# Hybrid decoder layer on one core: gemms by halves in one lasting PSUM layout, branch sums by accumulating transfers, late operand forms inside the first attention-output pair

## The chip, the core and the metric

The kernel runs on one core of one Trainium2 chip. The time is device microseconds of one execution, as the median of several runs. TensorE is called PE, VectorE DVE, ScalarE ACT, GpSimd POOL and the queue engine SyncE SP, as in the profile.

## What is computed

One layer of a hybrid decoder for 1024 prompt tokens and 8 sample tokens, model width 1024, all in float32. Three token mixers (a short gated convolution, a state-space scan "SSD", and a cross-attention into 256 memory tokens) read the same normalized input through one projection `w_in`; their outputs are weighted by gates, summed, multiplied by `w_merge_o` and added to the input; a gated feed-forward block and a last norm follow.

```python
def mixer_block(xn, ...):
    sc_b, sc_c, sc_x, z, xbc, dt_raw, q, gates = jnp.split(xn @ w_in, splits, axis=-1)
    ...
    y_a = (sc_b * conv_u) @ w_sc_out
    ...
    y_b = group_rmsnorm(y_ssd, ssm_norm_w, SSM_GROUPS) @ w_ssm_out
    ...
    y_c = jnp.einsum('bhlm,bmhd->blhd', probs, mem_v).reshape(bsz, seq, ATTN_DIM) @ w_attn_o
    g_a, g_b, g_c = jnp.split(jax.nn.sigmoid(gates), N_BRANCHES, axis=-1)
    merged = g_a * y_a + g_b * y_b + g_c * y_c
    return merged @ w_merge_o, (...)
```

## The kernel before

**Tiling.** Activations lie with features on 128 partitions and tokens along the free axis: eight tiles ("k-tiles") of 128 x 1032 for a width of 1024, where 1032 is the 1024 prompt columns and the 8 sample columns (`TT`; a half, `HT`, is 516). Every float32 operand of TensorE is split into a high and a low part (names that end in `h` and `l`: a cast on ACT, a subtraction on DVE, lines L167/168 for weights, L177/178 for activations, L254/255 and L393/395 in the pairs), and a product is three matmuls: high x high, high x low, low x high.

**Two kinds of products.** `gemm` (L199 to L219) multiplies one block of 128 output features: for each of the eight k-tiles and each of the three operand pairs it runs three matmuls of 260, 512 and 260 columns (`THIRDS`) into one PSUM tile of three banks, from a pool `pmm` of two such tiles. It is used 34 times: two z blocks early, eight q blocks (`q_step`), and 24 output blocks (`out_part`). The other kind is `strassen`, which does two output blocks at once, over halves of the tokens and of the features, with seven products of 24 matmuls in place of eight; its accumulators are three two-bank tiles m0, m1, m2 of a pool `pst`, and its matmuls have 256 and 260 columns. Its operands are combinations of tokens halves ("forms": B11, T1, nT2, B21, T3, B22, T4) and of weights (A, S, T, D: the weights' tiles are called `ao0A`, `ao0S` and so on for the pair `ao0`). The two PSUM pools do not fit side by side, so they are closed and opened in turn: gemms, pairs, gemms, pairs.

**Stages.** Up to 84 us norms and first products; 84 to 980 Strassen pairs for most of `w_in`; 980 to 1140 the q gemms; 1140 to 1551 the 24 output gemms; 1551 to 1655 the attention-output pairs `ao0`, `ao2`, `ao4`, `ao6`; 1655 to 1750 the merge product `pm` (16 blocks of 48 matmuls on half columns); then the feed-forward block.

**What sets the order.** Between the products of the q and output gemms the scan and then the attention run as small pieces: `tick` takes the next piece from a queue, `pace` says how many there are for each gemm, and `gemm` spreads them over its eight k-steps. `out_part(i, m)` runs in three passes of eight blocks m: i = 0 over the convolution branch, gated and written to DRAM as `mg_d`; i = 1 and i = 2 over the two halves of the scan branch, whose sum (L1497), gated (L1498), is written to DRAM as `yg_d`. `owed` holds that write until the next gemm. Each pass reads new operands `b00` to `b07`. The places where they change (`wo00`, `wo10`, `wo20`) are called seams here: `between`, called at each k of the gemm before, splits the first six, and the last two are split when the new pass begins.

**The sample attention.** Its last products are `pso` (L1665, 32 transfers of 1 KB to `os_d`); `s_back` reads them back as `osr` (SP, L1679), transposes them on TensorE into `psob` (L1682) and copies them into the last 8 columns of the eight raw attention tiles (L1685). The forms T1 and nT2 need these columns; after the last gemm (`wo27`) come T3, B22 and T4 (L1832, L1838 and the splits at L395), all in one block before `strassen` for `ao0` is called.

**The pairs and the sum of branches.** In each pair, in the hook `mid`, two gate tiles `gt3` and two tiles `yg` are loaded, and GpSimd adds `mg_d` into each `yg` by an accumulating transfer from DRAM. When the pair's products are done, VectorE multiplies by the gates (L1859, L1862, L1864) and adds `yg` (L1860, L1863, L1865):

```python
V.tensor_mul(oo[1][:, c1], oo[1][:, c1], gts[1][:, c1])
V.tensor_add(merged[m + 1][:, c1], oo[1][:, c1], ygs[1][:, c1])
V.scalar_tensor_tensor(oo[1][:, c0], pa, -1.0, gts[1][:, c0], op0=ALU.mult, op1=ALU.mult)
V.tensor_add(merged[m + 1][:, c0], oo[1][:, c0], ygs[1][:, c0])
```

Each engine and each queue runs its instructions in order; the tile layer puts in the waits and shifts instructions within limits. The merge's operands are the splits of the eight `merged` tiles (`mgs0` to `mgs7`).

## Time and profile before

| | |
|---|---|
| median of 3 runs | 2445.57 us (2440.04 to 2445.65) |
| profiled execution, its own time | 2446.0 us |
| its span | 2444.3 us |
| mean granted TensorE clock | 0.996 |
| attention-output stage, 1551 to 1655 | PE idle 15.3 of 104 us |
| merge matmuls `pm` | 1656.27 to 1750.25 us |
| q gemms, 980 to 1140 | PE idle 1.2 of 160 us |

The span is the time from the first to the last instruction of one profiled execution, and all positions in microseconds count from its start; the execution's own time is 1.7 us longer. Busy times of PE and of its weight loads (PEld) overlap. A row of the timeline or of the chain of waits gives a start, a duration, the engine, the line of the program and the tiles (out<-in). Durations of matmuls overlap with the next one's, so what a matmul costs is the step from one start to the next.

### The profile page before, as it was taken

The numbers are of one execution on the slowest core, as the hardware profiler recorded it, in microseconds if no ns is written. First come the engines' busy times: TensorE is split into PE (matmuls) and PEld (weight loads), VectorE is DVE, ScalarE is ACT, GpSimd is POOL, SyncE is SP. The second block draws the span as 40 slices with busy tenths as digits, with TensorE's granted clock in tenths as the row PEclk, the third lists the DMA queues.
The fourth block names the chain that finished last, engine by engine and source line by source line (L and its number), as shares of the span: only waits on it lengthen the run. The fifth ranks groups of instructions, "written<-read, shape, count | busy, mean of one in ns | idle before, by whom it ended". The sixth has DMA issues, their size and how long they took to land.

```text
span 2444.3 us, 45555 instructions
## 1 busy us (share of the span) xinstructions
PE 2394.4 (98%) x18812; PEld 2283.4 (93%) x18812; DVE 1647.5 (67%) x2688; ACT 1112.7 (46%) x1792; POOL 111.5 (5%) x171
## 2 busy tenths in 40 slices
PE   8999999999999999999999999899999999999998
PEld 7999999999999999888888887899999999999998
DVE  6744686777777775568687763764777655567865
ACT  6634555455454544657555442333543333343423
POOL 0000000000000000212211000000000000000000
PEclk9999999999999999999999999999999999999999
DMA  6444423444454346679796887575455332354622
GB/s 213 133 157 155 130 91 111 129 139 130 130 152 118 113 122 194 200 225 296 240 295 213 270 309 271 172 205 182 141 179 163 105 106 95 101 182 149 190 86 80
DMA packets 356678, 407.90 MB, mean 167 GB/s; under 512 B 15230, under 2 KB 276462, under 8 KB 356463
## 3 DMA queue, kind: packets, MB, share of 16 engines
q1 hardware_dynamic: 332182, 337.50, 45.0%
q10 hardware_dynamic: 23137, 63.26, 6.8%
q0 software_dynamic: 1152, 4.23, 0.9%
q8 instruction: 148, 2.42, 0.4%
q14 instruction: 59, 0.48, 0.1%
HBM read 288.81 MB, written 116.35 MB: 166 GB/s over the span
## 4 chain that ended last, share of the span: by engine, by line
PE 84%; DMA 6%; DVE 6%; ACT 1%; issue 1%; SPq 0%; DVEq 0%; ACTq 0%; POOLq 0%; POOL 0%
PE po L218 8%; PE pm L1934 4%; PE ps_q L218 3%; PE py L1063 1%; PE pss L1076 1%; PE ps_z L218 1%; DMA yg<-mg_d 1%; PE po L1055 1%; PE G16m L267 1%; PE d00m L267 1%; PE Z2m L267 1%; PE Z14m L267 1%; PE X18m L267 1%; PE Z10m L267 1%; PE Z6m L267 1%
## 5 line engine op out<-in xcount | busy, mean ns | idle before, releaser
L1007 ACT ACTIVATE r<-r,acum 128x128 f32<-128x128 f32 x256 | 79.3, 391 | 2.9 <-DMA r<-ac_d 2.1
L796 DVE SCALAR_TENSOR_TENSOR ax<-u,prm,ax 128x1024 f32<-128x1024 f32 x44 | 56.3, 1280 | 0.0
L948 ACT ACTIVATE st<-st,es 128x128 f32<-128x128 f32 x128 | 41.3, 392 | 22.4 <-DMA st<-in_state_ssm_dram 22.4
L1040 POOL TENSOR_TENSOR xdd<-xdt,decst 128x512 f32<-128x512 f32 x32 | 35.3, 1102 | 284.3 <-DVE xdt L1036 275.9
L1034 DVE TENSOR_TENSOR r<-r,cbm 128x1024 f32<-128x1024 f32 x32 | 39.1, 1223 | 4.3 <-ACT r L1009 2.4
L1059 DVE TENSOR_TENSOR y<-po,ea 128x512 f32<-128x512 f32 x28 | 19.3, 690 | 31.7 <-PE po L1055 31.7
L950 DVE SCALAR_TENSOR_TENSOR st<-sr,dts,st 128x128 f32<-128x128 f32 x128 | 40.3, 346 | 0.4
L1076 PE MATMUL pss<-xdd,bT 128*128 128x512 f32 x64 | 34.5, 620 | 2.2 <-ACT bT L1033 1.7
L954 DVE SCALAR_TENSOR_TENSOR sr<-st,sr 128x128 f32<-128x128 f32 x128 | 35.4, 286 | 1.1
L1063 PE MATMUL py<-r,xdt 128*64 128x128 f32 x512 | 35.0, 279 | 0.0
L1009 ACT ACTIVATE r<-r 128x1024 f32<-128x1024 f32 x32 | 33.8, 1058 | 0.7
L1949 DVE TENSOR_TENSOR x<-pm,xT 128x516 f32<-128x516 f32 x15 | 10.4, 694 | 34.1 <-PE pm L1934 34.1
L1089 POOL TENSOR_TENSOR s<-s,cdec 128x512 f32<-128x512 f32 x28 | 33.1, 1182 | 0.9 <-DVE s L1082 0.7
L1063 PEld LDWEIGHTS py<-r,xdt 128*64 128x64 f32 x512 | 27.3, 136 | 4.4 <-issue 1.0
L1055 PE MATMUL po<-bc,s 128*128 128x128 f32 x224 | 29.6, 275 | 0.0
L1055 PEld LDWEIGHTS po<-bc,s 128*128 128x128 f32 x224 | 28.0, 191 | 1.0
L1627 ACT ACTIVATE pr<-psa,mx 128x256 f32<-128x256 f32 x32 | 14.9, 471 | 30.2 <-DVE mx L1625 30.2
L799 DVE SCALAR_TENSOR_TENSOR ax<-u,prm,ax 128x1032 f32<-128x1032 f32 x22 | 28.3, 1286 | 0.0
L793 ACT ACTIVATE ax<-u,prm 128x1024 f32<-128x1024 f32 x22 | 27.4, 1246 | 1.7 <-DVE u L383 0.4
L1615 DVE SCALAR_TENSOR_TENSOR kc<-kc,qb 128x256 f32<-128x256 f32 x64 | 23.8, 419 | 5.6 <-DMA qb<-qs_d 5.4
L1036 DVE TENSOR_TENSOR xdt<-xp,dtT 128x512 f32<-128x512 f32 x32 | 21.9, 684 | 8.0 <-PE xp L1029 8.0
L1033 ACT COPY bT<-bp 128x128 f32<-128x128 f32 x32 | 8.4, 262 | 38.5 <-DVE cbm L1031 38.5
(9290 smaller groups left out, 9046.0 us busy)
## 6 DMA issues: line engine op xcount, KB each, us to landing
r<-ac_d SPq DMA_DIRECT2D x32, 512.0 KB
gt_d<-G ACTq DMA_DIRECT2D x24, 516.0 KB
gt<-gt_d SPq DMA_DIRECT2D x24, 516.0 KB
xs_d<-ax ACTq DMA_DIRECT2D x22, 516.0 KB
zs<-zs_d SPq DMA_DIRECT2D x16, 516.0 KB
yb_d<-x SPq DMA_DIRECT2D x16, 516.0 KB
in<-yb_d SPq DMA_DIRECT2D x16, 516.0 KB
st<-in_state_ssm_dram SPq DMA_DIRECT2D x32, 256.0 KB
```

The costliest lines, as they stand in the source:

```text
L218: PE.matmul(po, wt[:, ks], xc, start=(k == 0 and i == 0), stop=(k == nk - 1 and i == 2))
L267: PE.matmul(po, wt[:, ks], xc, start=(start and kt == 0 and i == 0), stop=(kt == 3 and i == 2), skip_group_check=True,)
L796: V.scalar_tensor_tensor(acc[:, :T], u[:, j : j + T], w[j], acc[:, :T], op0=ALU.mult, op1=ALU.add)
L948: S.activation(st[:, i], st[:, i], AF.Copy, scale=es[:, g * 4 + i, b : b + 1])
L950: V.scalar_tensor_tensor(st[:, i], rb, dts[:, g * 4 + i, b : b + 1], st[:, i], op0=ALU.mult, op1=ALU.add)
L954: V.scalar_tensor_tensor(rb, st[:, i], 1.0, rc, op0=ALU.mult, op1=ALU.mult, accum_out=ys[:, g * 4 + i, b : b + 1],)
L1007: S.activation(r[:, j, :], r[:, j, :], AF.Relu, scale=-1.0, bias=acum[:, c, h : h + 1])
L1034: V.tensor_tensor(r, r, bc(cbm.unsqueeze(1), [P, HPG, P]), op=ALU.mult)
L1055: PE.matmul(po[:, t * P : (t + 1) * P], state["s"][:, t * P : (t + 1) * P], bcg[1][:, cs], start=True, stop=True,)
L1063: PE.matmul(py[hp : hp + 64, (h // 2) * P : (h // 2 + 1) * P], xdt[:, h * 64 : (h + 1) * 64], r[:, (h % 2) * 4 + h // 2, :], start=True, s ...
L1076: PE.matmul(pss, bT, xdd, start=True, stop=True)
L1934: PE.matmul(po, wt[:, ks], x[:, half * HT + lo : half * HT + hi], start=(k == 0 and i == 0), stop=(k == KD - 1 and i == 2),)
```

## The change

It changes these things:

- **One PSUM layout.** The pool `pst` with m0, m1, m2 is opened once; gemms, pairs, merge and feed-forward take the three accumulators in turn from one deque `accs` (`next_ps`; `strassen` reverses it).
- **Gemms by halves.** `gemm` runs all eight k-tiles for the first 516 columns, then for the second, each product in two matmuls of 256 and 260 columns, so four for 1032 columns; the result is taken out by `put` in halves. Pieces are spread over 16 steps; `between` is called at every other one. The last output gemm (`wo27`) is `joint`: both halves in one pass over k, in two accumulators.
- **The start of the attention pairs.** The first weights of `ao0` are taken up before the forms T1 and nT2 and the last gemm. `s_back` comes one piece earlier.
- **Late forms.** The forms B22 and T4 are made after the T3 product of the first pair (`last_aforms`, called by `after_t3`).
- **Sums by transfers.** GpSimd adds `mg_d` into `yg_d` from DRAM to DRAM: blocks 0 to 3 at the start, 4 and 5, then 6 and 7 behind a pair's last transfer (`added`). For the pairs 0, 2 and 4 another accumulating transfer adds `yg_d` into `merged`; only the last pair loads `yg` and adds it on VectorE.

The core of the diff; not shown are the removal of `thirds` and of the old pools, the z blocks, which change as the q blocks do, and the callers that take `next_ps`:

```diff
@@ -196,27 +184,35 @@
 
     seam, owed = [], []
 
-    def gemm(w, acts, name, width=P, off=0):
-
-        hi, lo = w
-        ps = mm_ps(name)
+    def gemm(w, acts, name, put, joint=False):
+
         nk = len(acts)
         n = int(pace[0] + pace[1])
         pace[1] += pace[0] - n
-        marks = [nk * i // n for i in range(n)]
         between = seam.pop() if seam else None
-        for k, (ah, al) in enumerate(acts):
-            if between is not None:
-                between(k)
-            if k == 1 and owed:
-                owed.pop()()
-            for _ in range(marks.count(k)):
-                tick()
-            ks = slice(k * width + off, k * width + off + P)
-            for i, (wt, x) in enumerate(((hi, ah), (hi, al), (lo, ah))):
-                for po, xc in thirds(ps, x):
-                    PE.matmul(po, wt[:, ks], xc, start=(k == 0 and i == 0), stop=(k == nk - 1 and i == 2))
-        return ps
+        parts = ((0, 1),) if joint else ((0,), (1,))
+        marks = [len(parts) * nk * i // n for i in range(n)]
+        at = 0
+        for hs_ in parts:
+            pss = [next_ps(f"{name}{h}") for h in hs_]
+            for k, (ah, al) in enumerate(acts):
+                if between is not None and at % len(parts) == 0:
+                    between(at // len(parts))
+                if at == 2 and owed:
+                    owed.pop()()
+                for _ in range(marks.count(at)):
+                    tick()
+                at += 1
+                ks = slice(k * P, (k + 1) * P)
+                for i, (wt, x) in enumerate(((w[0], ah), (w[0], al), (w[1], ah))):
+                    for h, ps in zip(hs_, pss):
+                        for po, xc in halves_of(ps, x, h * HT):
+                            PE.matmul(
+                                po, wt[:, ks], xc, start=(k == 0 and i == 0), stop=(k == nk - 1 and i == 2),
+                                skip_group_check=True,
+                            )
+            for h, ps in zip(hs_, pss):
+                put(hv(ps), HS[h])
 
     def wblock(w, col):
...
         return pst[0].tile([P, 2, 512], F32, tag=tag, name=name)
+
+    def next_ps(name):
+        ps = st_ps(accs[0], name)
+        accs.rotate(-1)
+        return ps
 
...
             raw1, raw2 = st_raw(src1, f"{nm}r1"), st_raw(src2, f"{nm}r2")
-        tags = ("m0", "m1", "m2") if count[0] % 2 == 0 else ("m2", "m1", "m0")
-        count[0] += 1
+        tags = tuple(accs)
...
-    pmm[0] = mm_stack.enter_context(tc.tile_pool(name="pmm", bufs=2, space=PSUM))
+    pst_stack = ExitStack()
+    pst[0] = pst_stack.enter_context(tc.tile_pool(name="pst", bufs=1, space=PSUM))
 
 
...
         def s():
-            ps = proj(C_Q + i * P, f"q{i}")
             t = ev_tile(f"q{i}")
-            S.activation(t[:, :TT], flat(ps), AF.Copy, scale=QS)
+            proj(C_Q + i * P, f"q{i}", lambda ps, c: S.activation(t[:, c], ps, AF.Copy, scale=QS))
             G.tensor_copy(qs[:, i, :], t[:, T:TT])
             S.dma_start(q_d[i], t[:, :TT])
...
             out_ahead(nxt)
-        ps = gemm(weights(wblock(w, m * P), f"wo{nm}"), acts, f"po{nm}")
-        if i == 0:
-            V.tensor_mul(gt[:, :TT], flat(ps), gt[:, :TT])
-            owed.append(lambda: SY.dma_start(mg_d[m], gt[:, :TT]))
-        elif i == 1:
+        if i == 1:
             t = ev_tile(f"yr{nm}")
-            S.copy(t[:, :TT], flat(ps))
+
+        def put(ps, c):
+            if i == 0:
+                V.tensor_mul(gt[:, c], ps, gt[:, c])
+            elif i == 1:
+                S.copy(t[:, c], ps)
+            else:
+                V.tensor_tensor(t[:, c], ps, t[:, c], op=ALU.add)
+                V.tensor_mul(t[:, c], t[:, c], gt[:, c])
+
+        gemm(weights(wblock(w, m * P), f"wo{nm}"), acts, f"po{nm}", put, joint=nxt is None and m == KD - 1)
+        if i == 1:
             S.dma_start(yr_d[m], t[:, :TT])
         else:
-            V.tensor_tensor(t[:, :TT], flat(ps), t[:, :TT], op=ALU.add)
-            V.tensor_mul(t[:, :TT], t[:, :TT], gt[:, :TT])
-            owed.append(lambda: SY.dma_start(yg_d[m], t[:, :TT]))
+            dst, src_ = ((mg_d, yg_d)[i // 2][m], (gt if i == 0 else t)[:, :TT])
+            owed.append(lambda: SY.dma_start(dst, src_))
 
     split = []
...
             late += [[(s_out, b)], [(states[b],)] if b < 4 else []]
-        late += [[], [(s_back,)]]
+        late += [[(s_back,)]]
         pieces.extend([] for _ in range(at_ + len(late) - len(pieces)))
...
             run_next(outs)
+        wa = [wblock(a["w_attn_o"][0], m * P) for m in range(KD)]
+        ev_sums = lambda n: ev_tile(n, (P, 1024))
+        begun = st_begin(wa[0], wa[1], "ao0", ev_sums)
...
     fxo = fxo_stack.enter_context(tc.tile_pool(name="fxo", bufs=2))
     afx["T4"] = lambda part, nm: fxo.tile([P, 2, HT], F32R, tag=part, name=nm)
-    pst_stack = ExitStack()
-    pst[0] = pst_stack.enter_context(tc.tile_pool(name="pst", bufs=1, space=PSUM))
-    ev_sums = lambda n: ev_tile(n, (P, 1024))
-    wa = [wblock(a["w_attn_o"][0], m * P) for m in range(KD)]
-    begun = st_begin(wa[0], wa[1], "ao0", ev_sums)
     for kt in range(4):
         b12, b22 = raw8[kt][:, HS[1]], raw8[kt + 4][:, HS[1]]
         V.tensor_sub(b12, b22, b12)
         aform("T3", kt, b12)
-    for kt in range(4):
-        aform("B22", kt, raw8[kt + 4][:, HS[1]])
-    for kt in range(4):
-        t2, b21 = raw8[kt][:, HS[0]], raw8[kt + 4][:, HS[0]]
-        V.scalar_tensor_tensor(t2, t2, -1.0, b21, op0=ALU.mult, op1=ALU.subtract)
-        aform("T4", kt, t2)
+
+    def last_aforms():
+        for kt in range(4):
+            aform("B22", kt, raw8[kt + 4][:, HS[1]])
+        for kt in range(4):
+            t2, b21 = raw8[kt][:, HS[0]], raw8[kt + 4][:, HS[0]]
+            V.scalar_tensor_tensor(t2, t2, -1.0, b21, op0=ALU.mult, op1=ALU.subtract)
+            aform("T4", kt, t2)
 
     merged = []
     for m in range(0, KD, 2):
         oo = [ev_tile(f"ao{m}{i}")[:, :TT] if m == 0 else big(f"mg{m + i}") for i in range(2)]
-        gts, ygs = [], []
+        gts = []
+        for n in range(0 if m == 0 else m + 2, min(m + 4, KD)):
+            with nullcontext() if m == 0 else tc.issue_after(added):
+                G.dma_start(yg_d[n], mg_d[n], accum_op=ALU.add, max_dma_last_dim=TT)
+        if m == 6:
+            ygs = []
+            for i in range(2):
+                ygs.append(ev_tile(f"yg{m + i}")[:, :TT])
+                SY.dma_start(ygs[i], yg_d[m + i])
 
         def fetch():
             for i in range(2):
                 gts.append(ev_tile(f"gt3{m + i}")[:, :TT])
                 SY.dma_start(gts[i], gt_d[16 + m + i])
-                ygs.append(ev_tile(f"yg{m + i}")[:, :TT])
-                SY.dma_start(ygs[i], yg_d[m + i])
-                G.dma_start(ygs[i], mg_d[m + i], accum_op=ALU.add)
+
+        def first_out():
+            if m == 0:
+                last_aforms()
 
         pa = strassen(
             wa[m], wa[m + 1], aforms, f"ao{m}", ev_sums, lambda: tuple(t[:, c] for t in oo for c in HS),
-            begun=begun if m == 0 else None, mid=fetch,
+            begun=begun if m == 0 else None, mid=fetch, after_t3=first_out,
         )
         merged += oo if m else [big(f"mg{i}") for i in range(2)]
-        V.tensor_mul(oo[0], oo[0], gts[0])
-        V.tensor_add(merged[m], oo[0], ygs[0])
         c1, c0 = HS[1], HS[0]
-        V.tensor_mul(oo[1][:, c1], oo[1][:, c1], gts[1][:, c1])
-        V.tensor_add(merged[m + 1][:, c1], oo[1][:, c1], ygs[1][:, c1])
-        V.scalar_tensor_tensor(oo[1][:, c0], pa, -1.0, gts[1][:, c0], op0=ALU.mult, op1=ALU.mult)
-        V.tensor_add(merged[m + 1][:, c0], oo[1][:, c0], ygs[1][:, c0])
+        V.tensor_mul(merged[m], oo[0], gts[0])
+        V.tensor_mul(merged[m + 1][:, c1], oo[1][:, c1], gts[1][:, c1])
+        if m == 6:
+            V.tensor_add(merged[m], merged[m], ygs[0])
+            V.tensor_add(merged[m + 1][:, c1], merged[m + 1][:, c1], ygs[1][:, c1])
+        V.scalar_tensor_tensor(merged[m + 1][:, c0], pa, -1.0, gts[1][:, c0], op0=ALU.mult, op1=ALU.mult)
+        if m == 6:
+            V.tensor_add(merged[m + 1][:, c0], merged[m + 1][:, c0], ygs[1][:, c0])
+        else:
+            for i in range(2):
+                added = G.dma_start(merged[m + i], yg_d[m + i], accum_op=ALU.add).ins
     fxo_stack.close()
```

Three places where the order of instructions changes. The first is TensorE at the start of the attention pairs; `po` is the gemm's accumulator, `b07` its last operand, `wo27` the last weight block, `aB110` an operand form of the pair. Before:

```order
L1682 MATMUL psob<-ident,osr 128x8 x8
...
L218 MATMUL po_17065<-b07h,wo27l 128x260
L218 MATMUL po_17065<-b07h,wo27l 128x512
L218 MATMUL po_17065<-b07h,wo27l 128x260
L267 MATMUL ao0m_17210<-aB110ah,ao0Ah 128x256
L267 MATMUL ao0m_17210<-aB110ah,ao0Ah 128x260
```

And now:

```order
L210 MATMUL po_17787<-b07h,wo26l 128x260
L1665 MATMUL pso_17721<-vc_17646,pTs 32x256 x4
L1665 MATMUL pso_17721<-vc_17648,pTs 32x256 x4
L268 MATMUL ao0m_18066<-aB110ah,ao0Ah 128x256
...
L1682 MATMUL psob<-ident,osr 128x8 x8
L268 MATMUL ao0m_18066<-aB112al,ao0Ah 128x256
L268 MATMUL ao0m_18066<-aB112al,ao0Ah 128x260
...
L210 MATMUL po_17937<-b00h,wo27h 128x256
L210 MATMUL po_17937<-b00h,wo27h 128x260
L210 MATMUL po_17938<-b00h,wo27h 128x256
L210 MATMUL po_17938<-b00h,wo27h 128x260
```

Before, `psob` stood inside the last gemm and `ao0` behind it; now 20 matmuls of `ao0` stand ahead of `psob`, four more behind it, and then the whole last gemm, with two accumulators.

The second is TensorE at the last seam, where the operands `b00` to `b07` are new and `wo20` is the first weight block. Before:

```order
L218 MATMUL po_15617<-b07h,wo17l 128x260
L218 MATMUL po_15801<-b00h,wo20h 128x260
L218 MATMUL po_15801<-b00h,wo20h 128x512
L218 MATMUL po_15801<-b00h,wo20h 128x260
L218 MATMUL po_15801<-b00l,wo20h 128x260
```

And now:

```order
L210 MATMUL po_16364<-b07h,wo17l 128x260
L210 MATMUL po_16465<-b00h,wo20h 128x256
L210 MATMUL po_16465<-b00h,wo20h 128x260
L210 MATMUL po_16465<-b00l,wo20h 128x256
L210 MATMUL po_16465<-b00l,wo20h 128x260
```

Nine matmuls for each k-tile have become six of a half's columns, and `b01` follows after them.

The third is VectorE at the end of the pair `ao2`; `mg` are the branch sums, `gt` the gates, `ao4Sl` and `ao4Tl` operand parts of the next pair. Before:

```order
L381 TENSOR_TENSOR mg_17417<-mg_17417,ao2m_17422 128x516
L1862 TENSOR_TENSOR mg_17417<-mg_17417,gt_17544 128x516
L1863 TENSOR_TENSOR mg_17417<-mg_17417,yg_17546 128x516
L383 TENSOR_TENSOR mg_17416<-mg_17416,ao2m_17423 128x516
L1859 TENSOR_TENSOR mg_17416<-mg_17416,gt_17539 128x1032
L255 TENSOR_TENSOR ao4Sl<-ao4sa,ao4Sh 128x1024
L1860 TENSOR_TENSOR mg_17416<-mg_17416,yg_17541 128x1032
```

And now:

```order
L1869 TENSOR_TENSOR mg_18294<-mg_18294,gt_18420 128x516
L384 TENSOR_TENSOR mg_18293<-mg_18293,ao2m_18302 128x516
L1868 TENSOR_TENSOR mg_18293<-mg_18293,gt_18418 128x1032
L251 TENSOR_TENSOR ao4Sl<-ao4sa,ao4Sh 128x1024
L1873 SCALAR_TENSOR_TENSOR mg_18294<-ao2m_18301,gt_18420 128x516
L251 TENSOR_TENSOR ao4Tl<-ao4sb,ao4Th 128x1024
```

The adds of `yg`, and with them the instruction that waited for the transfer, no longer stand between the evacuations and the next pair's splits.

35 lines of the change are left out of this document (8 added, 27 removed).

## The prediction

> **What bounds the kernel now.** I read the head of the page first.
>
> ```profile
> span 2444.3 us, 45555 instructions
> PE 2394.4 (98%) x18812; PEld 2283.4 (93%) x18812; DVE 1647.5 (67%) x2688; ACT 1112.7 (46%) x1792; POOL 111.5 (5%) x171
> ```
>
> TensorE (PE) is busy for 2394.4 of 2444.3 us, so a change can win only where PE waits or runs at a low clock, and loses wherever it adds PE work. The table of busy time by stretches of the span (columns: length, then busy time and instructions of PE, weight load, VectorE, ScalarE, GpSimd, then granted clock, DMA share, GB/s) says where that is.
>
> ```profile
> 980.00:1140.00 160.00, 158.80 (x1141) 134.63 (x1140) 107.33 (x134) 96.55 (x201) 37.68 (x38) 1.00 0.72 230
> 1140.00:1270.00 130.00, 128.21 (x891) 109.18 (x890) 100.06 (x116) 70.65 (x135) 18.45 (x18) 1.00 0.85 274
> 1551.00:1655.00 104.00, 88.69 (x698) 85.96 (x696) 76.81 (x117) 36.40 (x60) 7.03 (x8) 0.96 0.71 192
> 1570.00:1575.00 5.00, 1.30 (x6) 1.31 (x7) 5.00 (x9) 3.43 (x5) 0.00 (x0) 0.74 0.27 53
> 1575.00:1580.00 5.00, 5.00 (x28) 5.00 (x28) 2.08 (x3) 0.11 (x1) 1.01 (x1) 0.58 1.04 325
> 1655.00:1660.00 5.00, 3.73 (x17) 3.73 (x18) 5.00 (x7) 1.31 (x2) 0.00 (x0) 0.50 0.40 121
> ```
>
> The query and output gemms (first two rows) are nearly gap-free: what they have is matmul time. The stage of the attention-output pairs, 1551 to 1655, has PE idle for 104 - 88.69 = 15.3 us, and twice the clock is low there or just behind: 0.74 and 0.58 in 1570 to 1580, 0.50 in 1655 to 1660. The list of waits (engine, line, what it waited for: sum, times, longest) from 1530 to 1660 names them; the VectorE row belongs to the same stretch.
>
> ```profile
> PE ao0m L267 <- ACT ao0Th L254: 5.0, 1, 5.0
> PE ao0m L267 <- DVE anT20al L395: 2.9, 1, 2.9
> PE pm L1934 <- DVE mg L383: 2.5, 1, 2.5
> PE ao4m L267 <- DVE ao4Sl L255: 1.6, 1, 1.6
> PE pm L1934 <- DVE wm01l L168: 1.4, 1, 1.4
> DVE mg L1863 <- DMA yg<-mg_d: 15.5, 4, 6.4
> ```
>
> The chain that ended last (start, us, what) shows why. I follow it from the last `pso` matmuls of the sample attention, at 1541.0.
>
> ```profile
> 1540.44 0.57 PE pso L1665 x8
> 1541.01 10.21 PE po L218 x64
> 1551.22 0.60 PE psob L1682 x8
> ...
> 1564.69 1.21 DVE aB220al L395 x2
> ...
> 1567.11 1.82 DVE at L1838 x3
> ...
> 1571.36 0.60 DVE ao0sb L299
> 1571.96 0.62 DVE ao0sb L300
> ...
> 1572.71 4.36 DMA yg<-yg_d
> ...
> 1637.15 6.68 DMA yg<-yg_d
> ...
> 1644.37 8.05 DMA yg<-mg_d
> ...
> 1655.00 1.23 DVE wm01l L168
> 1656.27 51.92 PE pm L1934 x416
> 1708.20 0.87 PE psf L1885 x4
> 1709.07 41.18 PE pm L1934 x347
> ```
>
> From `psob` to `ao0sb` VectorE works through the attention operand forms in one block (1551.82 to 1572.58) and PE's T3 product waits 5.0 us for its end. Later each pair ends with VectorE standing at L1863 until a GpSimd transfer has added `mg_d` into `yg`; the next pair's operand splits and the first evacuations are queued behind that instruction. The last such transfer ends at 1652.4 and decides when the merge matmuls `pm` start.
>
> **The change, part by part.** The sum goes against the profiled execution, 2446.0 us (span 2444.3), which is 0.4 us above the median of the runs, 2445.57.
>
> *Attention stage.* I compare the stretch from the last `pso` to the last `pm`: 1541.01 to 1709.07 + 41.18 = 1750.25, so 209.2 us. The PE work in it comes from these two rows and those above:
>
> ```profile
> 2132.64 19.99 PE u10m L267 x168
> 1396.79 0.63 PE L218 MATMUL po<-b04l,wo16h 128*128 128x260 f32 x3
> 1401.51 0.64 PE L218 MATMUL po<-b07h,wo16l 128*128 128x260 f32 x3
> ```
>
> An undisturbed Strassen pair of 168 matmuls on half columns takes 19.99 us, 0.119 each. In the gemm, ten groups of three start between 1396.79 and 1401.51: 4.72/10 = 0.472 us for 1032 columns. So: 76 `po` matmuls (64 in the row, 12 behind `psob`) 76/3 x 0.472 = 12.0; `psob` 0.7; four pairs 80.0; 16 merge blocks of 48, 768 x 0.119 = 91.4; `psf` 0.9. Together 185.0; idle time and low clock make up 24.2 us.
>
> Behind the change four things are gone. The PSUM pool is no longer exchanged between the last gemm and `ao0` (the 2.9 us before `ao0`, put down to `anT20al`; `ao0` started when the gemm's accumulator had been read). The B22 and T4 forms, from 1564.69 to 1571.36, 6.7 us of VectorE, come after T3's product (the 5.0 us, and with it the low clock of 1570 to 1580). Three pairs lose their adds and the VectorE wait for the transfer (1.6 us at `ao4`, with two smaller ones behind it). The last gemm, all of it, now lies between `psob` and the forms that need `psob`: 96 x 0.119 = 11.4 us of cover. The block of 20.8 us less the 6.7 leaves 14 us of VectorE, of which T3's forms and the weight sums (1.2 us) are needed only after the products nT2, T1 and B21.
>
> What is late next: `psob`. In its gemm's place ahead of it stand 20 matmuls of `ao0`, 20 x 0.119 = 2.4 us, and its operand goes out to memory and back:
>
> ```profile
> 1543.68 0.29 SPq L1679 DMA_DIRECT2D osr<-os_d x1
> ```
>
> Issue ends 3.0 us behind `pso`. The landing has no row; it lies between nothing and the 4.4 to 6.7 us of a 516 KB load (`yg<-yg_d`). I take 1.9 (32 KB is near the lower end): ready at 4.9, a stall of 2.5 us, ends 0.6 and 7.3. Queued behind `psob` on PE are the rest of B11 and the joint gemm, and no forms can start before it. I add 1.0 for the gemm's low weights, which VectorE splits behind the `psob` copies; 2.5 for T4 of the first pair (its forms, 6.7 us, run beside 96 matmuls, 11.4 us, but behind the T3 evacuations); 1.0 for pair 2, 0.7 for pair 6, 0.5 at `pm`. Together 8.2 of the 24.2 stay: **-16.0 us**, ends -10 and -20 (14 or 4 us stay).
>
> *Halves.* In 34 gemms each group of 1032 columns becomes four matmuls in place of three: 4 x 0.119 - 0.472 = 0.004 us, times 24 groups times 34: **+3.3 us**, ends 0 and 6 (both prices are good to about 0.003). The Trainium skill, page TensorE: Matmul & The Clock Gate (section "Wait — 56ns, not 53.3ns?"), gives a fixed 2.5 ns to each matmul; by that the 816 added ones would cost 2.0 us and the time would be 1.3 us lower; the trace's 4 ns is of that kind. The added evacuations (516 columns twice in place of 1032 once) lie beside the next half's matmuls, 6 us; without this cover each would cost about 0.1 us of VectorE start.
>
> *Seams.* With new operands a gemm's first half reads all eight k-tiles within 8 x 6 x 0.119 = 5.7 us, not 11.3 us. The operands come one by one (rows of TensorE, then of VectorE):
>
> ```profile
> 1418.89 0.63 PE L218 MATMUL po<-b00h,wo20h 128*128 128x260 f32 x3
> 1421.72 0.28 PE L1710 MATMUL psa<-kTh,q20h 128*128 128x256 f32 x1
> 1423.13 0.63 PE L218 MATMUL po<-b02h,wo20h 128*128 128x260 f32 x3
> ...
> 1422.33 1.23 DVE L178 TENSOR_TENSOR b04l<-in,b04h 128x1032 fp32r<-128x1032 f32 x1 [1.33 <-ACT b04h L177]
> 1423.60 1.24 DVE L178 TENSOR_TENSOR b05l<-in,b05h 128x1032 fp32r<-128x1032 f32 x1
> 1428.51 1.23 DVE L178 TENSOR_TENSOR b07l<-in,b07h 128x1032 fp32r<-128x1032 f32 x1
> ```
>
> At the last seam `wo20` starts at 1418.89; b04l is ready 4.7 us later (start plus step), and the new order asks for it after 4 x 0.71 + 0.24 = 3.1, so PE waits about 1.5; then 0.5 at b05, split next; then 24 score matmuls, which stand behind b05 and come at 12 in 1423.13 - 1421.72 = 1.4 us, give 2.8 us; b07l is ready 10.8 us after the start and costs 0.5 to 1.3. I take 3.3 there, 1.2 for the two earlier seams: **+4.5 us**, ends 0 and 12 (all of the 5.7 us that the first half is early, at two seams).
>
> *Pool exchange at 980.* The row 980 to 1140 has 1.2 us of PE idle; half of it I give to the exchange: **-0.6 us**.
>
> *Transfers.* Six accumulations into `yg` leave the path; eight between two DRAM tensors and six into `merged` take their place, on a GpSimd with nothing else to do.
>
> ```profile
> L1852 POOL DMA_DIRECT2D yg<-mg_d x8: 853/860/1011, 1578.0 to 1644.4; - x8
> DMA to landing us min/median/max: 6.0/7.3/8.2
> ```
>
> Each costs GpSimd 0.86 us of issue and lands after 7.3 us; a pair is 20 us long, so two of a kind lie beside the next pair: nothing, as long as the pair covers them. Without cover they cost what L1863 waited, up to 6.4 us each.
>
> Sum: -16.0 + 3.3 + 4.5 - 0.6 = -8.8; 2446.0 - 8.8 = 2437.2, and in terms of the median 2436.8: **2437 us**.
>
> **Rivals.** *The halves outrun their operands.* Two seams lose the full 5.7 us: 7.5 us above the sum, 2444, no change. For it: b04l to b07l come over 6 us, at the pace of their loads. Against it: the score matmuls fill part of it.
>
> *The wait only moves.* The accumulated `merged` tiles are first read by ScalarE's split for the merge; if that split stands in ScalarE's order ahead of pair 6's evacuations and the transfer is late, PE waits there as it did for L1863, up to 6.4 us: 2443. For it: ScalarE runs in order. Against it: 20 us of a pair for a 7.3 us landing.
>
> *Slower: the DRAM-to-DRAM sums are dear.* They move the same bytes in 512 pieces of 258 numbers, not 128 of 1032. If the cost goes by pieces, one lands after 4 x 7.3 = 29.2 us. The place is the last pair: `yg_d` 6 and 7 are issued behind pair 2's accumulations, and with T the end of `psob` that pair ends at T + 11.4 + 2 x 20 = T + 51.4, so at about T + 55; VectorE needs both back in SBUF at about T + 90, with a reload of 6.7. It decides from (35 - 6.7)/2 = 14 us each on; at 29.2 the merge starts 58.4 + 6.7 - 35 = 30 us later: 2467. For it: a write to memory that must be read first. Against it: bytes, not pieces, may set the landing. The Trainium skill, page DMA: Bandwidth & Descriptors (section "Anatomy of one DMA — SWDGE (gpsimd) path"), warns that completion takes longest where the target is HBM; its fit would give a 516 KB transfer 3.2 us, an estimate the trace's 7.3 already contradicts, so I keep the rows.
>
> *More gain.* Seams cost 0.5 and the stage keeps only 4 of its 24.2 us: -20.2 + 3.3 + 0.5 - 0.6 = -17.0: 2429. For it: the attention matmuls that stand between a gemm's products could cover each seam, and all of the T3 wait goes. Against it: nothing can shorten the way over `psob`.
>
> **How the numbers follow.** Forecast 0.50 (own range 2431 to 2442), halves outrun 0.13, wait moves 0.07, slower 0.12, more gain 0.18. Runs of this kernel can tell about 0.3% (7.3 us) from no change: the bounds are 2438.2 and 2452.9. Of the forecast's 0.50, 0.36 lie below 2438.2 and 0.14 within; with 0.18 of more gain, faster is 0.54. Within: 0.14 + 0.10 of the seams + 0.06 of the moved wait = 0.30. Slower: 0.12 + 0.03 + 0.01 = 0.16. The range goes from 2427 to 2451: the dear transfers (0.12) lie outside it, and the far ends of the rest.
>
> **What would show it.** In the table of stretches, the pair stage up to the merge should have PE idle for 5 to 10 us where it had 15.3, with no slice at half clock before T3; the list of waits should have no VectorE wait on a transfer and no `ao0Th` row of 5 us, but a new PE wait at `psob` near 2.5. The gemm should step 0.238 us per group of a half. At `wo00`, `wo10`, `wo20` rows of PE waiting for b04 to b07 should add up to about 4.5. The `yg_d` transfers should land in under 14 us. I am wrong if `psob` waits over 5 us and takes the clock with it, if the seam rows exceed 9 us, or if VectorE waits for `yg6` or `yg7` before `pm`.

## The result, and the profile after

The changed kernel takes 2447.27 us (median of 12 runs, 2443.57 to 2451.32) against 2445.06 (12 runs, 2439.99 to 2448.35): ratio 1.0012, 95% interval 1.0003 to 1.0022. It is a little slower, within the 0.3% that the prediction calls no change; the forecast was 2437.

The head of the page and some slices of the table of busy time (length, then PE, weight load, VectorE, ScalarE, GpSimd, then granted clock, DMA share, GB/s), changed kernel:

```profile
span 2445.5 us, 47220 instructions
PE 2399.7 (98%) x19628; PEld 2327.3 (95%) x19628; DVE 1646.4 (67%) x2703; ACT 1115.4 (46%) x1810; POOL 124.0 (5%) x177
```

```profile
980.00:1140.00 160.00, 157.02 (x1313) 141.62 (x1313) 101.19 (x128) 96.82 (x207) 41.48 (x37) 1.00 0.70 222
1430.00:1435.00 5.00, 3.25 (x21) 2.65 (x19) 3.24 (x3) 3.29 (x4) 0.00 (x0) 0.93 1.02 399
1435.00:1440.00 5.00, 4.38 (x19) 3.92 (x19) 3.86 (x4) 2.37 (x3) 0.00 (x0) 0.50 0.97 300
1440.00:1445.00 5.00, 5.00 (x40) 5.00 (x40) 4.33 (x15) 1.02 (x4) 0.00 (x0) 0.89 0.95 340
1560.00:1565.00 5.00, 5.00 (x30) 4.77 (x30) 4.85 (x14) 2.50 (x8) 0.00 (x0) 0.66 0.93 236
1620.00:1622.00 2.00, 2.00 (x11) 2.00 (x10) 0.59 (x1) 0.00 (x0) 0.85 (x1) 0.50 0.93 219
```

TensorE is busy 5.3 us longer in nearly the same span, and its low-clock slices have moved: they are at the last seam (0.93, 0.50, 0.89), behind `psob` (0.66) and at the end of pair 2 (0.50). The list of waits of TensorE, changed kernel (sum, times, longest):

```profile
PE ao2m L268 <- DVE mg L382: 6.1, 1, 6.1
PE xp L1029 <- DMA x<-xs_d: 5.3, 5, 1.6
PE psob L1682 <- DMA osr<-os_d: 2.5, 1, 2.5
```

The 5.0 us at T3, the 2.9 us before `ao0` and the two waits at `pm` are gone. In their place stands one wait of 6.1 us at `ao2`. The chain that ended last shows where it comes from:

```profile
1557.09 2.40 DMA osr<-os_d
...
1596.92 14.28 DMA ao4r<-in_w_attn_o_dram
...
1616.25 0.61 DVE mg L382
...
1616.91 5.41 PE ao2m L268 x24
1622.32 19.98 PE ao4m L268 x168
1642.30 19.97 PE ao6m L268 x168
1662.27 50.37 PE pm L1946 x420
```

A weight load for the next pair, `ao4r`, takes 14.28 us. VectorE stands in front of its first use, and the evacuation of `ao2`'s accumulator (L382), which TensorE needs, is queued behind. TensorE then works through its last 24 matmuls in 5.41 us instead of 2.86 at the low clock. In the kernel before, the same load was asked for at the first of these rows (its timeline: start, duration, engine) and used at the second, 7.1 us later, with VectorE waiting 0.33 us:

```profile
1588.73 0.38 SPq L248 DMA_DIRECT2D ao4r<-in_w_attn_o_dram  x1
...
1595.85 0.69 DVE L352 TENSOR_TENSOR ao4sa<-ao4r 128x512 f32<-128x512 f32 x1 [0.33 <-DMA ao4r<-in_w_attn_o_dram]
```

What runs beside the load now is on GpSimd's timeline of the changed kernel:

```profile
1592.50 0.89 POOL L1878 DMA_DIRECT2D mg<-yg_d  x1 [79.05 <-DVE mg L1868]
1594.85 0.84 POOL L1878 DMA_DIRECT2D mg<-yg_d  x1 [1.46 <-DVE mg L1873]
1595.39 2.39 POOL L1846 DMA_DIRECT2D yg_d<-mg_d  x2
```

Four accumulating transfers of 516 KB are issued within 5.3 us around the load, which is asked for at 1596.92; in the kernel before, one (1588.22) stood beside it. VectorE's timeline of the changed kernel shows what that costs it, 11.30 us of idle time:

```profile
1611.29 0.69 DVE L353 TENSOR_TENSOR ao4sa<-ao4r 128x512 f32<-128x512 f32 x1 [11.30 <-DMA ao4r<-in_w_attn_o_dram]
```

The difference by stretches of the two profiled executions (they end at the first q matmul, at the end of the last `pso` with `wo26` done, and at the end of `pm`; the difference is after minus before):

| stretch | before | after | difference | predicted |
|---|---|---|---|---|
| start to first q gemm | 981.2 | 982.3 | +1.1 | 0 |
| q and output gemms | 560.4 | 572.1 | +11.7 | +7.2 |
| attention output and merge | 208.6 | 200.2 | -8.4 | -16.0 |
| feed-forward and last norm | 694.1 | 690.8 | -3.2 | 0 |

The first line is within chance: in runs below whose program is alike up to there it lies between 978.2 and 982.3. The gemm stretch varies too, by about 4 us, among programs that are alike in it. The last stretch takes 691.9 to 694.1 us in the kernel before and the runs below with its gemms, 690.2 to 691.1 in the changed kernel, its variants and the run of halves in own tiles; the cause was not tested.

### The profile page after: what moved, and what is told of

It is laid out like the page before. It is cut to its first block, busy times and chain, and to the rows that moved or that the text cites. A ratio compares the mean times of both kernels' runs of the same rounds, so it can differ in the third digit from the quotient of the medians.

```text
span 2445.5 us, 47220 instructions
## 1 busy us (share of the span) xinstructions
PE 2399.7 (98%) x19628; PEld 2327.3 (95%) x19628; DVE 1646.4 (67%) x2703; ACT 1115.4 (46%) x1810; POOL 124.0 (5%) x177
## 4 chain that ended last, share of the span: by engine, by line
PE 84%; DVE 7%; DMA 6%; ACT 2%; issue 1%; SPq 0%; ACTq 0%; DVEq 0%
PE po L210 6%; PE pm L1946 4%; PE ps_q L210 3%; PE pd L2150 1%; PE py L1063 1%; PE pss L1076 1%; PE ps_z L210 1%; PE po L1055 1%; PE G16m L268 1%; PE d00m L268 1%; PE G12m L268 1%; PE Z14m L268 1%; PE C3m L268 1%; PE Z10m L268 1%; PE Z8m L268 1%
## 5 line engine op out<-in xcount | busy, mean ns | idle before, releaser
L1615 DVE SCALAR_TENSOR_TENSOR kc<-kc,qb 128x256 f32<-128x256 f32 x64 | 24.0, 417 | 11.2 <-DMA kc<-in_cache_mem_k_dram 7.5
L1491 DVE TENSOR_TENSOR yr<-po,yr 128x516 f32<-128x516 f32 x16 | 11.0, 692 | 26.1 <-PE po L210 22.3
L1029 PE MATMUL xp<-ident,x 128*128 128x128 f32 x128 | 21.2, 278 | 5.3 <-DMA x<-xs_d 5.3
```

## The experiments

Three questions: are the accumulating transfers what delays `ao4r`; what do the halves cost and by what; and what are the parts worth apart? "Gemms" and "pairs" are the second and third stretch of the table above (before 560.4 and 208.6, after 572.1 and 200.2), from the one profiled execution of each run. The ratio uses runs of the kernel before that were made beside each run, with medians of 2443.20 to 2444.49 us.

| run | base | median us | ratio to before, 95% | gemms | pairs |
|---|---|---|---|---|---|
| sums early | after | 2440.56 | 0.9987 (0.9978 to 0.9997) | 574.9 | 195.2 |
| forms early | after | 2452.09 | 1.0033 (1.0021 to 1.0045) | 575.6 | 206.2 |
| seams joint | after | 2445.11 | 0.9998 (0.9987 to 1.0009) | 573.9 | 200.6 |
| adds on VectorE | after | 2449.61 | 1.0021 (1.0010 to 1.0032) | 571.3 | 206.1 |
| sums early, seams joint | after | 2438.65 | 0.9977 (0.9968 to 0.9986) | 570.1 | 194.6 |
| sums in large pieces | after | 2446.97 | 1.0009 (1.0000 to 1.0018) | 571.8 | 201.0 |
| late forms alone | before | 2442.65 | 0.9997 (0.9988 to 1.0006) | 556.6 | 209.4 |
| early sums alone | before | 2438.55 | 0.9980 (0.9972 to 0.9989) | 571.1 | 197.3 |
| late forms and early sums | before | 2433.88 | 0.9958 (0.9944 to 0.9971) | 565.7 | 191.7 |
| the same, four sums held | before | 2432.16 | 0.9954 (0.9938 to 0.9970) | 561.8 | 194.2 |
| the same, two sums held | before | 2438.10 | 0.9970 (0.9958 to 0.9982) | 566.7 | 193.2 |
| halves in own tiles | before | 2458.66 | 1.0060 (1.0047 to 1.0073) | 570.7 | 212.7 |

### The sums moved away from the load

```diff
-        for n in range(0 if m == 0 else m + 2, min(m + 4, KD)):
+        for n in ((0, 1, 2, 3, 4, 5), (), (6, 7), ())[m // 2]:
```

Sums 4 and 5, which stood beside `ao4r`, go to the start; 6 and 7 wait for pair 2.

> The changed kernel, but the sums of yg_d 4 and 5 are issued with 0 to 3 during the output gemms, so that no transfer between two DRAM tensors stands in the pair ao2. Theory 'contention': in the changed kernel the second load of ao4's weights (ao4r) was issued at 1596.9, landed 14.3 us later, and VectorE stood 11.3 us at ao4sa with ao2's evacuations behind it (PE wait 6.1 us, then 24 matmuls at low clock, 5.4 instead of 2.9 us). If the two sums caused it, ao4r lands in about 7 us, the 6.1 us wait and the low clock go, and the time falls by about 8 us, to a ratio of about 0.998 of before. Theory 'late chain': the late forms delay the release of the weights' buffer (issue at 1596.9); then the PE wait stays at 4 us or more and the time falls by under 3 us.

Waits of TensorE in this run, then its chain:

```profile
PE ao0m L268 <- DVE yr L1491: 3.2, 1, 3.2
PE ao2m L268 <- DVE mg L382: 1.4, 1, 1.4
```

```profile
1600.05 9.59 DMA ao4r<-in_w_attn_o_dram
...
1615.35 3.13 PE ao2m L268 x24
```

With two accumulations fewer beside it the load takes 9.59 us, the wait at `ao2` falls from 6.1 to 1.4 and its last matmuls take 3.13 us: 5.0 us in the stretch. So the sums delay that load. Over the runs its time goes with their number: from issue to use it takes about 7 us beside one (the kernel before), 9 to 10 beside two, 14 to 15 beside four. A new wait of 3.2 us stands where the scan's partial result `yr` is now read late; that an early sum causes it is not shown.

### The pieces of the sums

```diff
-                G.dma_start(yg_d[n], mg_d[n], accum_op=ALU.add, max_dma_last_dim=TT)
+                G.dma_start(yg_d[n], mg_d[n], accum_op=ALU.add, max_dma_last_dim=4 * TT)
```

> The changed kernel with the sums between DRAM tensors in 128 pieces of 1032 numbers instead of 512 of 258. Theory 'the price goes by bytes': the sums land after 9 to 17 us as before, ao4's second weight load again takes about 14 us, the wait of 6 us in ao2 stays, time within 2 us of the changed kernel. Rival 'the price goes by pieces' (my rival of the prediction): landing near 7 us, the wait falls under 2 us, 6 to 8 us faster.

Its wait at `ao2`:

```profile
PE ao2m L268 <- DVE mg L382: 6.7, 1, 6.7
```

Four times longer pieces change neither the time nor this wait; the load takes 14.89 us. The sums themselves land a little sooner (8.8/11.2/17.4 us, shortest, median and longest, become 5.8/9.3/15.0). So the price goes mostly by bytes, not by pieces. The transfer tables give it. First the changed kernel from 1590 to 1620, then this run in the same window, then the kernel before from 1578 to 1610, where the transfers add into SBUF (queue, packets, MB, share of 16 engines):

```profile
q1 hardware_dynamic: 4448, 3.61, 42.9%
q0 software_dynamic: 1344, 2.11, 40.4%
```

```profile
q0 software_dynamic: 576, 2.11, 35.6%
```

```profile
q0 software_dynamic: 576, 2.11, 37.0%
```

The accumulating queue takes 0.404 x 30 x 16 / 2.11 = 92 engine-us (microseconds of one of the 16 engines) for each MB with 1344 packets, 0.356 x 30 x 16 / 2.11 = 81 with 576, and 0.370 x 32 x 16 / 2.11 = 90 in the kernel before. The plain loads beside them take 0.429 x 30 x 16 / 3.61 = 57 in the changed kernel.

### The late forms undone

```diff
+    last_aforms()
     merged = []
...
-            if m == 0:
-                last_aforms()
+            pass
```

> The changed kernel with B22 and T4 forms made ahead of the first pair again (late forms undone). Theory 'contention': the wait of 6.1 us in ao2 moves little, since it hangs on the two sums between DRAM tensors, and a wait of some 5 us before T3 of ao0 comes back: slower than the changed kernel by 3 to 6 us. Theory 'late chain': VectorE frees the weights' buffer of ao4 earlier and the 6.1 us wait shrinks under 2 us, which pays for the T3 wait: within 2 us of the changed kernel.

```profile
PE ao2m L268 <- DVE mg L382: 6.2, 1, 6.2
PE ao0m L268 <- ACT ao0Th L250: 4.8, 1, 4.8
```

The wait at T3 is back (4.8 us; it was 5.0) and the stretch is 6.0 us longer, while the wait at `ao2` stays. The two are independent here, and the late forms are worth 6.0 us of the stretch, 4.8 of them the wait.

### The seams in one pass

```diff
-... put, joint=nxt is None and m == KD - 1)
+... put, joint=m == 0 or (nxt is None and m == KD - 1))
```

The gemms `wo00`, `wo10` and `wo20` read their operands at the old rate.

> The changed kernel, but the first gemm of each output pass (wo00, wo10, wo20) does both halves in one pass over k, as wo27 does: the seams' operands are needed at the old pace, everything else stays. Theory 'halves outrun their operands at the seams': the PE waits at b04 to b07 of wo20 (1.0 + 0.8 + 0.5 us) and the low clock behind them (about 3 us) go: 4 to 6 us faster than the changed kernel in the stretch up to pso. Rival 'seams are small, the loss of 11.7 us between 981 and 1554 is spread over all gemms (dearer groups, waits for x and vc loads)': under 2 us faster.

```profile
PE pso L1665 <- DMA vc<-in_cache_mem_v_dram: 4.8, 5, 2.8
PE psa L1710 <- ACT pr L1627: 3.4, 2, 2.2
```

The waits for b04 to b07 are gone, but these two are longer instead, and the gemm stretch is not shorter. The median is 2.2 us under the changed kernel's, less than expected. One profiled execution, here the slowest of the 12, does not tell these two waits from chance. With early sums the same edit gave 1.9 us (2440.56 to 2438.65), and there the intervals of the ratios overlap:

> The changed kernel with the sums 4 and 5 early and wo00, wo10, wo20 in one pass. The two gains add if they are in different places: 6.7 + 2.2 us below the changed kernel, about 2438.5 us, ratio near 0.998. Rival: the first gains nothing where the seams' stretch is bound by loads that the early sums delay; then no more than 6 us below the changed kernel.

### The shares added on VectorE

Each pair loads `yg` and adds it on VectorE as before, with the accumulating transfers `yg<-mg_d`; the layout, the halves and the late forms of the change stay. Core of the edit:

```diff
+                G.dma_start(ygs[i], mg_d[m + i], accum_op=ALU.add)
...
+        V.tensor_mul(oo[0], oo[0], gts[0])
+        V.tensor_add(merged[m], oo[0], ygs[0])
```

> The changed kernel with the branch sums as in the kernel before: yg loaded to SBUF, GpSimd adds mg_d there, VectorE adds the result; no transfer between DRAM tensors. Theory 'the sums by transfers are worth it': VectorE waits for yg at the end of each pair again (15.5 us in the kernel before, PE waits of 3 to 4 us at ao4 and 4 us and a low clock before pm): 4 to 8 us slower than the changed kernel. Rival 'they only moved the wait': the 6.1 us in ao2 and the low clock behind it (together 8.6 us) go and the waits at ao4 and pm come back for about as much: within 3 us of the changed kernel.

```profile
PE ao4m L268 <- DVE mg L384: 1.7, 1, 1.7
...
PE pm L1937 <- ACT mgs6h L165: 1.6, 1, 1.6
```

The 6.1 us at `ao2` are gone and the waits of the kernel before are back, 5.9 us longer in the stretch, 2.3 us in the median, less than the 4 to 8 expected. The sums by transfers were thus worth at most a little as they stood (the intervals of the two ratios to before overlap), and more where they harm no load.

### The halves on the kernel before

```diff
+        for hs_ in parts:
+            pss = [pmm[0].tile([P, 2, 512], F32, tag="mm", name=f"{name}{h}") for h in hs_]
...
-    pmm[0] = mm_stack.enter_context(tc.tile_pool(name="pmm", bufs=2, space=PSUM))
+    pmm[0] = mm_stack.enter_context(tc.tile_pool(name="pmm", bufs=3, space=PSUM))
```

`gemm` and `put` are the change's, with `wo27` by halves too; the pools are still exchanged, and forms and sums are the old ones.

> The kernel before with its exchange of PSUM pools and all else unchanged, but each gemm by halves as in the change, in two-bank tiles of its own, three in turn. It mends the run in three-bank tiles, where the two halves share a bank. Theory 'the halves cost the 11.7 us' (first q gemm to last pso: 560.4 us before, 572.1 changed): this stretch is 9 to 13 us longer than before, and the kernel slower by about that, ratio near 1.0045. Rival 'only the fourth matmul costs, 4.9 us; the rest came with the sums in DRAM, the layout or the moved pieces': 4 to 6 us slower.

```profile
PE xp L1035 <- DMA x<-xs_d: 4.7, 5, 1.6
PE ao0m L275 <- DVE yr L1503: 6.3, 1, 6.3
```

The gemm stretch in the kernel before, then here (columns as in the table of busy time):

```profile
980.00:1541.00 561.00, 548.80 (x3810) 468.30 (x3808) 378.55 (x599) 287.20 (x578) 70.35 (x68) 1.00 0.78 255
979.00:1550.00 571.00, 555.22 (x4549) 507.31 (x4549) 382.75 (x618) 287.36 (x595) 77.12 (x68) 1.00 0.75 250
```

+10.3 us in the gemm stretch (9 to 13 expected), at full clock. TensorE's idle time is +3.6 of it (12.2 to 15.8), and the rest is busy time. The 744 added matmuls are 3 to 4 us; what the other 2 to 3 us of busy time are was not isolated. The rest of its loss, 4.1 us in the pairs, holds the 6.3 us wait for `yr`. So the halves cost about what the whole change loses in its gemms, without any of its other parts.

Two earlier attempts at this price failed. Both kept the old tile of three banks. In one the two halves shared the middle bank, in the other (both halves in one pass, four matmuls for each k-tile) two open accumulations did, and it does not compute the layer's output. They took 2550.21 and 2529.87 us, ratios 1.0442 (1.0426 to 1.0458) and 1.0351 (1.0334 to 1.0367). Why was not isolated, and neither says anything about the price of a half.

```diff
+        f = mm_ps(name).rearrange("p n c -> p (n c)")
...
+                        for lo, hi in ((0, 256), (256, HT)) if h == 0 else ((HT, 768), (768, TT)):
+                            po, xc = f[:, 256 + lo : 256 + hi], x[:, lo:hi]
```

> The kernel before, with its own three-bank accumulators and everything else unchanged, but each gemm runs the first 516 columns over all eight k-tiles and then the second, in two matmuls each, and is taken out by halves. Theory 'the halves cost the 11.7 us' (stretch from the first q gemm at 981 to the last pso: 560.4 us before, 572.1 changed): this kernel is 9 to 13 us longer in that stretch and slower than before by about that, ratio near 1.0045. Rival 'only the fourth matmul costs (744 x 0.0054 = 4 us); the rest came with the sums, the layout or the moved pieces': 3 to 5 us slower.

> The kernel before with four matmuls instead of three for each product of its gemms, both halves in each k-step, so that the order over k and the pace of the pieces stay as they were. Theory 'four matmuls cost what their step shows': 34 x 24 groups x 0.0054 = 4.4 us slower than before, no new waits at b04 to b07 of wo20. If halves run in order cost 9 to 13 us and this one 4.4, the difference is the price of the order; rival 'the order costs nothing': both alike.

### The other parts on the kernel before

Late forms alone: `after_t3=last_aforms if m == 0 else None` in the old kernel, gemms and adds unchanged.

> The kernel before with one change: B22 and T4 forms made behind the T3 product of the first attention pair. Theory 'late forms remove the T3 wait': the wait of 5.0 us at ao0Th and the low clock behind it (about 3 us) go, so 4 to 8 us faster, ratio near 0.998, if nothing else ends later. Rival 'the forms only move': VectorE reaches the next pair's weight sums and the yg adds later, PE waits in ao0's T4 or ao2 instead, and the gain is under 2 us.

```profile
PE ao4m L267 <- DVE mg L383: 4.4, 1, 4.4
```

The wait at T3 is gone and nothing is gained: the pairs start earlier and wait for `yg<-mg_d` instead (4.4 us at `ao4`, where it was 0.9 and 0.8). Early sums alone, with the transfers into `merged`:

```diff
+        for n in ((0, 1, 2, 3, 4, 5), (), (6, 7), ())[m // 2]:
+            with nullcontext() if m == 0 else tc.issue_after(added):
+                G.dma_start(yg_d[n], mg_d[n], accum_op=ALU.add, max_dma_last_dim=TT)
...
-        V.tensor_add(merged[m], oo[0], ygs[0])
...
+                added = G.dma_start(merged[m + i], yg_d[m + i], accum_op=ALU.add).ins
```

> The kernel before with the sums by transfers alone (blocks 0 to 5 early), forms made where they were. Late forms alone gained nothing (0.9997), the end of each pair then waited for yg instead. Theory 'the two parts hide each other': here the T3 wait of 5 us and its low clock (3 us) stay, the waits behind yg go (1.6 + 0.9 + 0.8 + 2.5 + 1.4 us and a low clock of about 2 us before pm): 6 to 9 us faster. Rival 'each part gains only with the other': under 3 us.

-11.3 us in the pairs, though T3 waits as before (5.0 us). In this profiled execution, the slowest of the 11, most of it is given back in the gemms (+10.7, where `pso` waits for its loads 6.7 us, 1.5 before); the median keeps 5.9 us (2438.55 against 2444.49 for the kernel before, run beside it). The two edits together:

> The kernel before (gemms of three matmuls, exchanged pools) with the other two parts of the change: late forms and sums by transfers, blocks 0 to 5 early. Theory 'the attention stage's gain does not need the halves': the T3 wait and the VectorE waits for yg go together, the 2.9 us of the pool exchange stays; last pso to last pm 209.2 before, about 195 here, and nothing lost before: 12 to 16 us faster than before, ratio near 0.994. Rival 'without the last gemm behind psob the forms are late': VectorE's 14 us of forms have no cover, PE waits in ao0 instead, and the gain is under 8 us.

Waits and chain of this run:

```profile
PE ao0m L267 <- DVE anT20al L395: 2.9, 1, 2.9
PE pso L1665 <- DMA vc<-in_cache_mem_v_dram: 6.2, 2, 5.2
```

```profile
1586.80 8.90 DMA ao4r<-in_w_attn_o_dram
```

The pairs take 191.7 us, 16.9 less than before. That is as much as the forecast's gain of the stage, without the halves, though not by the same terms: the 2.9 us of the pool exchange stay, and there is no wait at `psob`. The kernel is 0.42% faster, 10.6 us in the median where 12 to 16 were expected; in this execution the gemms take 5.3 us more. What is left is a wait of 5.2 us for a load of the attention's values `vc`, which now lies beside the first sums. If sums delay what runs beside them, holding some of them until `psob` must free that load and delay a later one. A small GpSimd copy that reads `psob`'s result does it:

```diff
+            back.append(G.tensor_copy(gate, raw8[3][:, T:TT]).ins)
...
-            with nullcontext() if m == 0 else tc.issue_after(added):
+            with nullcontext() if n < 2 else tc.issue_after(back[0] if m == 0 else added):
```

> The kernel with late forms and sums by transfers on the gemms of before, but the sums 2 to 5 wait for psob (a small GpSimd copy of a psob column stands ahead of them in its queue). Theory 'the sums delay the loads they run beside': the wait of 5.2 us for vc goes, the stretch from the first q gemm to wo27 falls back from about 565 to 560.4 us, and four sums have the 26 us until ao2's load; total 3 to 5 us below the run with early sums, about 2430 us, ratio near 0.994. Rival 'that wait was variation': same as the early sums within 1.5 us, or slower by a new wait in ao2 if four sums behind psob delay ao2's and ao4's loads.

```profile
PE pso L1666 <- DMA vc<-in_cache_mem_v_dram: 1.7, 1, 1.7
PE ao0m L267 <- DVE yr L1497: 6.2, 1, 6.2
```

With `n < 4` in its place only two are held:

> The same, with only the sums 4 and 5 held back until psob; 2 and 3 run during the output gemms. Theory 'the sums delay the loads they run beside': the wait at 1488 us came with the sum of block 2, so it stays, and this run is near the one with early sums (2433.9 us), 2 us or more above the one with four held. Rival: alike with four held.

```profile
PE pso L1666 <- DMA vc<-in_cache_mem_v_dram: 4.2, 2, 3.7
```

Four held: the wait for `vc` falls from 6.2 to 1.7 us, and one of 6.2 for `yr` comes up at `ao0`, where the run without holding had the 2.9 us at `anT20al`. Two held: a sum still lies beside the load of `vc`, most of its wait stays (4.2), and the 6.2 at `yr` come all the same; its median is 4 us above that of the run with none held, where it was expected near it. The delay of `vc` goes with the sums beside it. The 6.2 us do not go with the number held. Both runs have the small copy, whose tile comes from the same buffers as `yr`, and in both the last load of `yr` is issued only behind `psob` (SyncE's waits, four held):

```profile
SPq L1485 <- PE psob L1683: 3.7, 1, 3.7
```

So this wait may be the price of the copy and not of holding. But the own-tiles run has one like it (6.3) without a copy, and the cause stays open. The version with four held (2432.16) and the one with none (2433.88) are not told apart; both beat both kernels.

## Why the prediction failed, point by point

**The matmuls of the halves: right.** 3.3 us were put down, from 4 x 0.119 against 0.472. The changed kernel's timeline of TensorE gives the step in two rows ahead of the last seam (the three behind them are for the next point):

```profile
1407.43 0.40 PE L210 MATMUL po<-b02h,wo16h 128*128 128x256 f32 x2
...
1411.48 0.40 PE L210 MATMUL po<-b07h,wo16l 128*128 128x256 f32 x2
...
1432.81 0.51 PE L210 MATMUL po<-b04h,wo20h 128*128 128x256 f32 x2 [0.99 <-ACT b04h L165]
...
1434.08 0.65 PE L210 MATMUL po<-b04l,wo20h 128*128 128x256 f32 x2 [0.76 <-DVE b04l L166]
...
1436.58 0.80 PE L210 MATMUL po<-b05l,wo20h 128*128 128x256 f32 x2 [0.47 <-DVE b05l L166]
```

17 groups of a half in 4.05 us, 0.2382, so 2 x 0.2382 - 0.472 = 0.0045 in place of 0.004: 3.7 us. The expectations above reckon with 0.0054; the rows do not tell the two apart. The fixed 2.5 ns to a matmul of the Trainium skill (page TensorE: Matmul & The Clock Gate, section "Wait — 56ns, not 53.3ns?") is about half of what an added matmul cost here, 4.5 ns.

**The seams: the place right, the clock missed.** At `wo20` TensorE waits three times, in the last three rows above. With a smaller one (0.2 us) that is 2.4 us, not the 3.3 assumed, and the two earlier seams, put at 1.2, have none. But the clock falls to 0.50 behind them. The three slices shown above lose 4.38 x 0.50 + 3.25 x 0.07 + 5.00 x 0.11 = 3.0 us of TensorE time. The sum, 5.4, is near the 4.5 by another way: the number was luck.

**Not in the sum at all: `x<-xs_d`.** The scan's transposes wait 5.3 us for their loads, 1.7 before: +3.6. The changed kernel, its variants and the halves in own tiles have 4.5 to 5.7, the runs with the old gemms 0.7 to 2.4. So it comes with the halves; by what was not settled. Other waits are shorter: TensorE's whole idle time in the gemm stretch grew by about 3 us.

**`psob`: right, its clock missed.** A wait of 2.5 us was put down and 2.5 came (the operand landed 2.40 us after its issue began). The slice behind it, 1560 to 1565, runs at 0.66, 5.00 x 0.34 = 1.7 us more.

**Late forms, and pairs without the wait for a transfer: right.** T3 waits for nothing, the pairs 4 and 6 take 19.98 and 19.97 us against the 19.99 assumed, and `pm` starts without a wait.

**Transfers: the step that failed.** The prediction put accumulations at "nothing, as long as the pair covers them". It asked when their own result is needed, also in the rival, which it placed in the last pair. There nothing happened. But the four transfers around 1595 stood beside a load, which took 14.28 us in place of 7.1, and an in-order engine stood for it: 6.1 us of wait, and 5.41 - 2.86 = 2.5 us of low clock behind it, where 1.0 was put down for pair 2. That is 7.6 us more, as much as lies between -16.0 and -8.4. That it fits so exactly is chance: 1.7 us of clock behind `psob` were not in the sum, while the splits of the low weights and T4's forms together cost about 1.2 us, not 3.5, and the 1.2 put down for pair 6 and `pm` did not come. The run with early sums took 5.0 us of it away by moving two of them; the old gemms with late forms and early sums reached -16.9. None of the prediction's three signs of being wrong came up, since none of them looks at this load. Its mark for the sums, landings under 14 us, did fail (the sums into `yg_d`, issue to landing):

```profile
DMA to landing us min/median/max: 8.8/11.2/17.4
```

**The pool exchange at 980: not seen.** TensorE's idle time in 980 to 1140 went from 1.2 to 3.0 us with the new waits, so a gain of 0.6 would not show.

So the stage gave 8.4 us of 16, the gemms took 11.7 instead of 7.2, and 3.2 us came from a place that was not in the sum. The rival of halves that outrun their operands named the right mechanism for a part of it, at another size; no rival had a load delayed by the sums.

## What to carry to other kernels

Price a transfer that is taken off the critical path by the loads it will run beside and by the in-order engine that stands for them, not by when its own result is needed. A gemm that runs its halves one after the other asks for its operands twice as fast: here that cost 5.4 us of waits and low clock at one seam in the profiled execution, but only about 2 us of the median came back when the old pace was restored there. Try the parts of a change apart and in pairs: late forms alone gave nothing (0.9997), early sums alone 0.9980, both 0.9958, since each alone leaves a wait that the other removes. The halves, the layout and the new start that they came with cost more than they gave: with early sums in both, 2440.56 against 2433.88 us.

## What the runs showed of the hardware

Three waits of 0.99, 0.76 and 0.47 us within 5 us were followed by a clock of 0.50. In the kernel before, one wait of 2.9 us was not followed by a lower clock (the two slices around it, 1553 to 1557 and 1557 to 1562):

```profile
1553.00:1557.00 4.00, 1.08 (x7) 0.74 (x6) 4.00 (x21) 1.51 (x9) 0.00 (x0) 1.00 0.69 204
1557.00:1562.00 5.00, 5.00 (x41) 4.83 (x41) 5.00 (x8) 2.04 (x4) 0.00 (x0) 1.00 0.44 158
```

In the own-tiles run the seam kept its clock, so waits at a seam do not always bring the fall (a slice of it, with 1.48 us of idle time):

```profile
1430.00:1435.00 5.00, 3.52 (x25) 2.90 (x24) 3.84 (x4) 4.61 (x6) 0.00 (x0) 1.00 0.94 318
```

The Trainium skill, page TensorE: Matmul & The Clock Gate, warns of gaps over some 3.4 us (section "HAM oscillation — how this bites in real kernels"), and in the section "A second HAM failure mode: psum-queue depth-cycling" of frequent short ones. The seam, where no wait reached 1 us, agrees with the second. The 2.5 us at `psob`, under that length, were followed by 0.66 all the same, so the length of a gap alone did not decide here. Accumulating transfers took 81 to 92 engine-us for each MB against 57 for the plain loads beside them in the changed kernel. Pieces four times longer took about a tenth less of the engines and did not change the kernel's time.
